# Value products of head pairs on alternating halves of the array, in four attentions, and a division moved behind a sum

## The chip, the core and the metric

One core of a Trainium2 chip runs one program from first load to last store. The metric is the device time of an execution in microseconds, median over runs; smaller is better. TensorE (PE in the profile) multiplies, VectorE (DVE), ScalarE (ACT) and GpSimd (POOL) work element by element, and SyncE (SP) issues most transfers. Each engine works through its own queue in a fixed order and waits on semaphores of the others.

## The reference

256 tokens of width 1024 pass through two transformer blocks. The first has a layer with a sparse attention of three branches (compressed, selected, windowed; 16 heads of 64 columns), a layer with a dilated attention, and a feed-forward part in each. The second block has a feed-forward part, a mixer (an index-selected attention of 8 heads, a memory attention of 4, and a state-space layer), and another feed-forward part. The part that the change touches is the end of every attention, the product of probabilities with values. In the dilated one, three groups of keys (dilations 1, 4 and 16) are joined by their log-sum-exp:

```python
def dilated_attention(h, w_q, k_shared, v_shared, w_out, rel_bias):
    ...
    for gi, (window, dilation) in enumerate(DILATIONS):
        o, lse = dilated_group_attention(q[:, :, gi], k_shared[:, :, gi], v_shared[:, :, gi], dilation, window, rel_bias)
        ...
    alpha = jax.nn.softmax(jnp.stack(lses, axis=-1), axis=-1)
    o = jnp.einsum('bsgrdi,bsgri->bsgrd', jnp.stack(outs, axis=-1), alpha)
    return o.reshape(B, S, D_MODEL).astype(h.dtype) @ w_out
```

Joined so, each head's output is the sum over the three groups of unnormalised weights times values, divided by one sum of all weights.

## The kernel before

Activations lie transposed: 128 channels on the partitions, 256 tokens along the row. Projections (`mm3`, L228 to L230) split each float32 operand into a high and a low part and make three matmuls of 128 x 128 by 128 x 256 for each block of 128 channels.

An attention works on pairs of heads. For each head the scores of two blocks of 128 queries come out of TensorE into a PSUM bank of the pool "sc" (two banks; L635 in the first attention, L766 in the dilated one). VectorE adds the position bias, keeps the row minimum and writes the result to a buffer `z` of 128 x 384 (L644, L769; one operation for 128 keys, one for 256). ScalarE makes the exponential in place and sums it (L647, L775). `pv_transposed` (L451 to L453) turns z into three blocks in a bank of the pool "tr" (two banks), and ScalarE, once in four calls of the first attention VectorE, copies them to `pt` (L458 or L456). `pv_mm` then multiplies: V is the stationary operand, 64 columns wide, so that head i of a pair fills partitions 64 i to 64 i + 63 of the output bank; two matmuls, one with 256 moving columns (L465) and one with 128 (L466). Each is in float32 and takes two passes, which are two records in the trace. Before the transposition VectorE multiplies z by the reciprocal of the sum (in the dilated attention two operations for each z, L786 and L787; z has nine buffers). At the end `split_act` splits the sum of a pair into high and low parts (L263 on ScalarE, L264 on VectorE) for the output projection.

In the first attention (`nsa`) a pair's products stand in the order head 0 branch 0, head 0 branch 1, head 1 branch 0, head 1 branch 1, and a full-width product of the compressed branch closes the bank (L694). In the dilated attention `values(h)` does one head, so three products of head 0 (one for each dilation) come before three of head 1. The index attention in `mixer` has one product for each head, and the memory attention two of 256 columns (L1196).

The program's text doesn't fix the order of the queues. A scheduler that knows dependencies and buffers moves instructions; so projections of later heads and, towards the end of an attention, the output projection stand between the attention's steps in TensorE's queue. The compression's hidden layer (`hidden`, L580) is the one place where the kernel before writes products for both halves in alternation.

Of the kernel before, what the change touches and what calls it, by code (L numbers as in the profile page):

```python
# [11 lines left out]
F32 = mybir.dt.float32  # L12
F32R = mybir.dt.float32r
AF = mybir.ActivationFunctionType
ALU = mybir.AluOpType
# [106 lines left out]
class Builder:  # L122
# [344 lines left out]

    def evac_k(self, dst, ps, R):
        self.nc.vector.tensor_tensor(dst, ps, R, ALU.mult)
# [30 lines left out]
    def nsa(self, xs, first):  # L500
# [6 lines left out]
        with ExitStack() as es:  # L507
# [173 lines left out]
            def values(g, st, j):  # L681

                den = st["den"][:, 2 * j:2 * j + 2]
                nc.vector.reciprocal(den, den)
                nc.vector.tensor_tensor(den, den, Gv[:, :, 4 * g + 2 * j:4 * g + 2 * j + 2, 1:3].rearrange("p t h b -> p h b t"), ALU.mult)
                Op = self.bank("ov")[:, :S]
                for i in range(2):
                    for br in range(2):
                        z = st["P"][2 * j + i, br]
                        nc.vector.tensor_scalar(z[:, 0:128], z[:, 0:128], den[:, i, br, 0:1], None, ALU.mult)  # L690
                        nc.vector.tensor_scalar(z[:, 128:384], z[:, 128:384], den[:, i, br, 1:2], None, ALU.mult)
                        pt = self.pv_transposed(ap, z, br + 2 * i)
                        self.pv_mm(Op, i, [Vs[:, br, tb, 64 * g:64 * g + 64] for tb in range(2)], pt, br == 0, False)
                nc.tensor.matmul(Op, Vc[:, g, 2 * j:2 * j + 2, :].rearrange("p i d -> p (i d)"), st["pc"], start=False, stop=True, skip_group_check=True)  # L694
                O.append(self.split_act(Op, "o", 2 * g + j, flip=True))
# [36 lines left out]
    def dilated(self, xs):  # L732
        nc, tc, A = self.nc, self.tc, self.A
        (XK, XQ), R, r = self.norm_all(xs, ["kv_norm", "norm_mix1"])
        with tc.tile_pool(name="dil", bufs=1) as ap:
# [5 lines left out]
            Q, O, Z, Op = {}, [], {}, [None]  # L741
# [38 lines left out]
            def values(h):  # L780
                g, i = h // 4, h % 2
                zs, rden = Z.pop(h)
                if i == 0:
                    Op[0] = self.bank("ov")[:, :S]
                for d, z in enumerate(zs):
                    nc.vector.tensor_scalar(z[:, 0:128], z[:, 0:128], rden[:, 0:1], None, ALU.mult)  # L786
                    nc.vector.tensor_scalar(z[:, 128:384], z[:, 128:384], rden[:, 1:2], None, ALU.mult)  # L787
                    pt = self.pv_transposed(ap, z, d)
                    self.pv_mm(Op[0], i, [V[:, d, tb, 64 * g:64 * g + 64] for tb in range(2)], pt, d == 0, d == 2)
                if i:  # L790
                    O.append(self.split_act(Op[0], "o", h // 2, flip=True))
# [11 lines left out]
            for h in range(17):  # L803
                if h < 16:
                    scores(h)
                    if h % 4 < 3 and h < 12:
                        queries(h // 4 + 1, h % 4)
                if h:
                    values(h - 1)
# [275 lines left out]
    def mixer(self, xs):  # L1085
# [4 lines left out]
        with ExitStack() as es:  # L1090
# [81 lines left out]
            for p in range(2):  # L1172
# [9 lines left out]
                V.reciprocal(st[:, 1], st[:, 1])  # L1182
                for i in range(2):
# [9 lines left out]
                    o = Op[64 * i:64 * i + 64]  # L1193
                    for kb in range(2):
                        h = 2 * p + i
                        nc.tensor.matmul(o, MV[:, kb, 64 * h:64 * h + 64], pt[:, kb * S:kb * S + S], start=(kb == 0), stop=(kb == 1), skip_group_check=True)  # L1196
# [24 lines left out]
            for p in range(4):  # L1221
# [15 lines left out]
                V.reciprocal(st[:, 1, :], st[:, 1, :])  # L1237
                for i in range(2):
# [3 lines left out]
                    pt = self.pv_transposed(ap, z, i, 512)  # L1242
                    self.pv_mm(Op, i, [VA[:, tb, :] for tb in range(2)], pt, True, True)
# [163 lines left out]
```

## Time and profile before

| what | us |
|---|---|
| median of 3 runs | 1373.02 (1370.69 to 1375.62) |
| the profiled execution, its time | 1374.24 |
| its span in the trace | 1372.4 |
| PE busy, share of the span | 1349.5, 98% |
| VectorE busy | 1020.7, 74% |
| ScalarE busy | 743.8, 54% |
| GpSimd busy | 186.8, 14% |

The rows come from four views: the page (engine totals and 40 slices of the span), the busy time of each engine by stretch, groups of instructions by line and shape, and the timeline of single instructions. A start in the timeline is where the record starts; a matmul's end is modelled and overlaps its follower, so spacing is read from one start to the next. Before the change the first attention's value products lie between 76 and 147 us, the dilated one's between 424 and 548, the memory and index attentions' between 1083 and 1135.

### The profile page before, as it was taken

What the parts mean: (1) busy time and instruction counts of PE and PEld (TensorE: products, weight loads), DVE (VectorE), ACT (ScalarE), POOL (GpSimd) and SP (SyncE); (2) the same over time, 40 slices, a digit from 0 to 9 for tenths busy, and PEclk for the clock granted to TensorE, in tenths of its full rate; (3) what the DMA queues carried; (4) which work ended last, traced back from release to release, by engine and by line L of the source; (5) the groups of instructions that cost most, each with busy time, mean ns of one, the idle gap of its engine ahead of it and who ended that gap; (6) DMA issues with size and microseconds to landing.
All of it is one profiled execution on the core that took longest, in us unless ns stands there. A gap on an engine that the chain in (4) does not pass through costs nothing.

```text
span 1372.4 us, 27451 instructions
## 1 busy us (share of the span) xinstructions
PE 1349.5 (98%) x10880; PEld 1277.6 (93%) x10880; DVE 1020.7 (74%) x2207; ACT 743.8 (54%) x1406; POOL 186.8 (14%) x225
## 2 busy tenths in 40 slices
PE   8999999999999999999999999999999999999997
PEld 8887999999999887899999999999987879999997
DVE  7888677766799874999954877756598797777643
ACT  4677555545668775664544555544333665554442
POOL 4200100001210000332100310001031044000011
PEclk8999999999999999999999999999999999999998
DMA  9751355546764440456755466556744254555461
GB/s 285 250 177 35 105 195 189 188 139 196 235 214 139 139 139 2 146 192 216 237 192 189 160 209 203 188 169 186 237 131 146 78 169 155 183 188 188 151 197 47
DMA packets 227120, 232.76 MB, mean 170 GB/s; under 512 B 5944, under 2 KB 221184, under 8 KB 226992
## 3 DMA queue, kind: packets, MB, share of 16 engines
q1 hardware_dynamic: 223392, 226.14, 51.9%
q10 hardware_dynamic: 3600, 4.88, 1.0%
q8 instruction: 85, 1.39, 0.4%
q14 instruction: 43, 0.35, 0.1%
HBM read 226.69 MB, written 4.30 MB: 168 GB/s over the span
## 4 chain that ended last, share of the span: by engine, by line
PE 55%; DVE 4%; issue 1%; ACT 1%; DMA 1%; POOL 0%; POOLq 0%; DVEq 0%; ACTq 0%
PE mm L228 7%; PE mm L230 7%; PE mm L229 7%; PE tr L230 4%; PE sc L230 4%; PE sc L229 4%; PE tr L228 4%; PE sc L228 4%; PE tr L229 4%; PE ov L229 2%; PE ov L230 2%; PE ov L228 2%; PE ov L1007 1%; DVE wl L188 1%; DMA mem<-in_memT_dram 1%
## 5 line engine op out<-in xcount | busy, mean ns | idle before, releaser
L187 ACT ACTIVATE wh<-raw 128x1024 fp32r<-128x1024 f32 (+2 forms) x405 | 417.9, 1036 | 452.8 <-PE mm L229 157.1
L188 DVE TENSOR_TENSOR wl<-raw,wh 128x1024 fp32r<-128x1024 f32 (+2 forms) x405 | 489.7, 1211 | 162.6 <-ACT wh L187 157.9
L228 PE MATMUL mm<-xh,wh 128*128 128x256 f32 x952 | 271.9, 286 | 1.6 <-ACT wh L187 1.4
L230 PE MATMUL mm<-xh,wl 128*128 128x256 f32 x952 | 271.2, 285 | 1.0 <-DVE wl L188 1.0
L229 PE MATMUL mm<-xl,wh 128*128 128x256 f32 x952 | 270.1, 284 | 0.0
L228 PEld LDWEIGHTS mm<-xh,wh 128*128 128x128 f32 x952 | 182.1, 191 | 7.1 <-issue 5.0
L230 PEld LDWEIGHTS mm<-xh,wl 128*128 128x128 f32 x952 | 181.2, 190 | 4.8 <-issue 3.1
L229 PEld LDWEIGHTS mm<-xl,wh 128*128 128x128 f32 x952 | 181.6, 191 | 2.5 <-issue 2.4
L293 POOL TENSOR_TENSOR sqacc<-sqacc,sq 128x256 f32<-128x256 f32 x60 | 60.8, 1016 | 613.5 <-ACT sq L292 336.4
L228 PE MATMUL sc<-xh,wh 128*128 128x256 f32 x464 | 129.8, 280 | 1.9 <-ACT wh L187 1.9
L229 PE MATMUL sc<-xl,wh 128*128 128x256 f32 x464 | 129.6, 279 | 0.0
L230 PE MATMUL sc<-xh,wl 128*128 128x256 f32 x464 | 129.3, 279 | 0.0
L228 PE MATMUL tr<-xh,wh 128*128 128x256 f32 x440 | 123.2, 280 | 0.4 <-ACT wh L187 0.4
L230 PE MATMUL tr<-xh,wl 128*128 128x256 f32 x440 | 123.3, 280 | 0.2 <-DVE wl L188 0.2
L229 PE MATMUL tr<-xl,wh 128*128 128x256 f32 x440 | 123.1, 280 | 0.0
L228 PEld LDWEIGHTS sc<-xh,wh 128*128 128x128 f32 x464 | 87.7, 189 | 2.1 <-ACT wh L187 2.1
L229 PEld LDWEIGHTS sc<-xl,wh 128*128 128x128 f32 x464 | 87.7, 189 | 0.0
L230 PEld LDWEIGHTS sc<-xh,wl 128*128 128x128 f32 x464 | 87.2, 188 | 0.0
L228 PEld LDWEIGHTS tr<-xh,wh 128*128 128x128 f32 x440 | 83.4, 189 | 0.6 <-ACT wh L187 0.6
L229 PEld LDWEIGHTS tr<-xl,wh 128*128 128x128 f32 x440 | 83.5, 190 | 0.0
L230 PEld LDWEIGHTS tr<-xh,wl 128*128 128x128 f32 x440 | 83.1, 189 | 0.4 <-DVE wl L188 0.4
L228 PE MATMUL ov<-xh,wh 128*128 128x256 f32 x224 | 62.6, 280 | 0.0
(483 smaller groups left out, 3467.2 us busy)
## 6 DMA issues: line engine op xcount, KB each, us to landing
raw<-in_ffn_w_up_dram SPq DMA_DIRECT2D x44, 1024.0 KB, 5.3
raw<-in_ffn_w_in_dram SPq DMA_DIRECT2D x44, 1024.0 KB, 5.2
raw<-in_w_in_dram SPq DMA_DIRECT2D x17, 1024.0 KB, 5.4
raw<-in_ffn_w_down_dram SPq DMA_DIRECT2D x16, 1024.0 KB, 5.3
raw<-in_ffn_w_out_dram SPq DMA_DIRECT2D x16, 1024.0 KB, 5.9
raw<-in_b_w_q_dram SPq DMA_DIRECT2D x12, 1024.0 KB, 5.2
raw<-in_a_w_in_dram SPq DMA_DIRECT2D x8, 1024.0 KB, 8.6
bt<-u_scratch SPq DMA_DIRECT2D x28, 256.0 KB, 3.8
```

The costliest lines, as they stand in the source:

```text
L187: nc.scalar.activation(hv, v, AF.Copy)
L188: nc.vector.tensor_tensor(lv, v, hv.bitcast(F32), ALU.subtract)
L228: nc.tensor.matmul(ps, sh, mh, start=(i == 0), stop=False)
L229: nc.tensor.matmul(ps, sh, ml, start=False, stop=False)
L230: nc.tensor.matmul(ps, sl, mh, start=False, stop=(i == n - 1))
L293: nc.gpsimd.tensor_tensor(acc[:, 0], acc[:, 0], s, ALU.add)
L1007: nc.tensor.matmul(o, self.s5_zc[:, s, c, :], x, start=(i == 0), stop=(i == 3), tile_position=(0, 32 * b))
```

## The change

Three things are done. A new function `pv_pair` takes both heads' `pt` and issues, for each block of keys, head 0 and then head 1, that is, left half and right half of the array in turn. The first, the index and the memory attention call it (or the same order written out) once both heads' blocks are transposed. In the dilated attention `values` now handles a pair: the two heads' transpositions of the next dilation are written ahead of the products of this one, z is no longer multiplied by the reciprocal, and at the end the two reciprocals are spread over 64 partitions each by four small matmuls, copied to `Rd` by ScalarE, and multiplied into the sum by VectorE (`od`), which is then split. `Rd` and `od` come from the two "kt" buffers that the query evacuation also uses.

```diff
+    def pv_pair(self, O, V, pts, start, stop):
+
+        nc = self.nc
+        for kb, (q0, q1, c0) in enumerate(((0, 256, 0), (128, 256, 256))):
+            for i, pt in enumerate(pts):
+                nc.tensor.matmul(O[64 * i:64 * i + 64, q0:q1], V[kb], pt[:, c0:c0 + q1 - q0], start=(start and kb == 0), stop=(stop and kb == 1), skip_group_check=True)
...
-                for i in range(2):
-                    for br in range(2):
+                ptss = []
+                for br in range(2):
+                    pts = []
+                    for i in range(2):
                         z = st["P"][2 * j + i, br]
                         nc.vector.tensor_scalar(z[:, 0:128], z[:, 0:128], den[:, i, br, 0:1], None, ALU.mult)
                         nc.vector.tensor_scalar(z[:, 128:384], z[:, 128:384], den[:, i, br, 1:2], None, ALU.mult)
-                        pt = self.pv_transposed(ap, z, br + 2 * i)
-                        self.pv_mm(Op, i, [Vs[:, br, tb, 64 * g:64 * g + 64] for tb in range(2)], pt, br == 0, False)
+                        pts.append(self.pv_transposed(ap, z, br + 2 * i))
+                    ptss.append(pts)
+                for br in range(2):
+                    self.pv_pair(Op, [Vs[:, br, tb, 64 * g:64 * g + 64] for tb in range(2)], ptss[br], br == 0, False)
...
-            def values(h):
-                g, i = h // 4, h % 2
-                zs, rden = Z.pop(h)
-                if i == 0:
-                    Op[0] = self.bank("ov")[:, :S]
-                for d, z in enumerate(zs):
-                    nc.vector.tensor_scalar(z[:, 0:128], z[:, 0:128], rden[:, 0:1], None, ALU.mult)
-                    nc.vector.tensor_scalar(z[:, 128:384], z[:, 128:384], rden[:, 1:2], None, ALU.mult)
-                    pt = self.pv_transposed(ap, z, d)
-                    self.pv_mm(Op[0], i, [V[:, d, tb, 64 * g:64 * g + 64] for tb in range(2)], pt, d == 0, d == 2)
-                if i:
-                    O.append(self.split_act(Op[0], "o", h // 2, flip=True))
+            def values(p):
+
+                g = p // 2
+                (z0, r0), (z1, r1) = Z.pop(2 * p), Z.pop(2 * p + 1)
+                Op = self.bank("ov")[:, :S]
+
+                def turned(d):
+                    return [self.pv_transposed(ap, z[d], 0) for z in (z0, z1)]
+
+                pts = turned(0)
+                for d in range(3):
+                    nxt = turned(d + 1) if d < 2 else None
+                    self.pv_pair(Op, [V[:, d, tb, 64 * g:64 * g + 64] for tb in range(2)], pts, d == 0, d == 2)
+                    pts = nxt
+                ps = self.bank("tr")[:, :S]
+                for tb in range(2):
+                    for i, r in enumerate((r0, r1)):
+                        nc.tensor.matmul(ps[64 * i:64 * i + 64, tb * P:tb * P + P], r[:, tb:tb + 1].to_broadcast([P, 64]), self.ident, start=True, stop=True, skip_group_check=True)
+                Rd = ap.tile([P, S], F32, name=self.n("Rd"), tag="kt", bufs=2)
+                nc.scalar.activation(Rd, ps, AF.Copy)
+                o = ap.tile([P, S], F32, name=self.n("od"), tag="kt", bufs=2)
+                nc.vector.tensor_tensor(o, Op, Rd, ALU.mult)
+                O.append(self.split_act(o, "o", p, flip=True))
...
-            for h in range(17):
-                if h < 16:
-                    scores(h)
-                    if h % 4 < 3 and h < 12:
-                        queries(h // 4 + 1, h % 4)
-                if h:
-                    values(h - 1)
+            for h in range(16):
+                scores(h)
+                if h % 4 < 3 and h < 12:
+                    queries(h // 4 + 1, h % 4)
+                if h and h % 2 == 0:
+                    values(h // 2 - 1)
+            values(7)
```

The memory and the index attention are changed in the same manner: both heads' `pt` first, then key block by key block with the heads in turn.

What the scheduler made of it is shown by the built order of both kernels. TensorE in the first attention, the products of one head pair (`pt` are the transposed probabilities, `Vsw` the values of both branches); before:

```order
L465 MATMUL ov_1155<-pt_1162,Vsw 64x256
L466 MATMUL ov_1155<-pt_1162,Vsw 64x128
L465 MATMUL ov_1155<-pt_1172,Vsw 64x256
L466 MATMUL ov_1155<-pt_1172,Vsw 64x128
L465 MATMUL ov_1155<-pt_1182,Vsw 64x256
L466 MATMUL ov_1155<-pt_1182,Vsw 64x128
L465 MATMUL ov_1155<-pt_1192,Vsw 64x256
L466 MATMUL ov_1155<-pt_1192,Vsw 64x128
L694 MATMUL ov_1155<-pc_870,Vc 128x256
```

and after:

```order
L473 MATMUL ov_1155<-pt_1162,Vsw 64x256
L473 MATMUL ov_1155<-pt_1170,Vsw 64x256
L473 MATMUL ov_1155<-pt_1162,Vsw 64x128
L473 MATMUL ov_1155<-pt_1170,Vsw 64x128
L473 MATMUL ov_1155<-pt_1178,Vsw 64x256
L473 MATMUL ov_1155<-pt_1186,Vsw 64x256
L473 MATMUL ov_1155<-pt_1178,Vsw 64x128
L473 MATMUL ov_1155<-pt_1186,Vsw 64x128
L705 MATMUL ov_1155<-pc_870,Vc 128x256
```

Before, pt_1162 and pt_1172 are head 0 and the other two head 1; after, neighbours in the list are head 0 and head 1.

TensorE near the end of the dilated attention, one dilation of one head pair, with the output projection (`oh`, `ol`) around it. Before, one head's product and the next one's transposition:

```order
L465 MATMUL ov_6777<-pt_6855,Vd 64x256
L466 MATMUL ov_6777<-pt_6855,Vd 64x128
L451 MATMUL tr_6871<-con,z_6761 128x128
L452 MATMUL tr_6871<-con,z_6761 128x128
L453 MATMUL tr_6871<-con,z_6761 128x128
```

and after:

```order
L473 MATMUL ov_6800<-pt_6817,Vd 64x256
L230 MATMUL sc_6966<-oh_6582,wl_6963 128x256
L228 MATMUL sc_6966<-oh_6720,wh_6962 128x256
L229 MATMUL sc_6966<-ol_6721,wh_6962 128x256
L451 MATMUL tr_6835<-con,z_6743 128x128
L452 MATMUL tr_6835<-con,z_6743 128x128
L453 MATMUL tr_6835<-con,z_6743 128x128
L473 MATMUL ov_6800<-pt_6823,Vd 64x256
L473 MATMUL ov_6800<-pt_6817,Vd 64x128
L473 MATMUL ov_6800<-pt_6823,Vd 64x128
```

The pair's four products stand in two pieces: head 0 with 256 columns by itself, then, behind other work, the other three.

## Rows read from the trace of the kernel before

**Rows 1.** The page: engine totals, and the granted clock of TensorE in 40 slices.
```profile
PE 1349.5 (98%) x10880; PEld 1277.6 (93%) x10880; DVE 1020.7 (74%) x2207; ACT 743.8 (54%) x1406; POOL 186.8 (14%) x225
...
PEclk8999999999999999999999999999999999999998
```

**Rows 2.** Busy time by stretch (length, then PE, PEld, DVE, ACT, POOL, clock, DMA, GB/s).
```profile
60.00:147.00 87.00, 85.85 (x626) 70.08 (x625) 69.53 (x279) 60.55 (x181) 6.98 (x14) 1.00 0.36 115
108.00:120.00 12.00, 10.96 (x70) 7.57 (x70) 10.96 (x54) 10.07 (x40) 0.91 (x3) 1.00 0.27 88
424.00:548.00 124.00, 123.20 (x876) 101.68 (x876) 88.82 (x346) 86.46 (x266) 0.48 (x2) 1.00 0.35 101
548.00:600.00 52.00, 46.45 (x362) 44.27 (x362) 50.58 (x162) 34.56 (x61) 20.98 (x28) 0.93 0.49 157
```

**Rows 3.** Groups by shape, TensorE, whole span: dilated (Vd) and first attention (Vsw).
```profile
L465 PE MATMUL ov<-pt,Vd 128*64 128x256 f32 x96 | 30.3, 403 | 0.3 <-ACT pt L458 0.3
...
L465 PE MATMUL ov<-pt,Vsw 128*64 128x256 f32 x64 | 17.2, 397 | 0.0
```

**Rows 4.** Timeline (start, length, engine, line) of TensorE, one call, dilated attention.
```profile
430.92 0.28 PE L229 MATMUL mm<-xl,wh 128*128 128x256 f32 x1
431.04 0.28 PE L230 MATMUL mm<-xh,wl 128*128 128x256 f32 x1
431.25 0.65 PE L465 MATMUL ov<-pt,Vd 128*64 128x256 f32 x2
431.73 0.38 PE L466 MATMUL ov<-pt,Vd 128*64 128x128 f32 x2
432.04 0.33 PE L451 MATMUL tr<-con,z 128*128 128x128 f32 x1
```

**Rows 5.** Timeline of TensorE, four calls of a head pair, first attention.
```profile
96.14 0.38 PE L466 MATMUL ov<-pt,Vsw 128*64 128x128 f32 x2
96.36 0.65 PE L465 MATMUL ov<-pt,Vsw 128*64 128x256 f32 x4
96.79 0.44 PE L466 MATMUL ov<-pt,Vsw 128*64 128x128 f32 x4
97.07 0.59 PE L465 MATMUL ov<-pt,Vsw 128*64 128x256 f32 x2
97.50 0.38 PE L466 MATMUL ov<-pt,Vsw 128*64 128x128 f32 x2
```

**Rows 6.** Timeline of TensorE, two heads next to each other, index attention.
```profile
1120.44 0.66 PE L465 MATMUL ov<-pt,VA 128*64 128x256 f32 x4
1120.93 0.40 PE L466 MATMUL ov<-pt,VA 128*64 128x128 f32 x4
1121.25 0.70 PE L1232 MATMUL sc<-KA,qa 128*128 128x256 f32 x2
```

**Rows 7.** Timeline of TensorE, the hidden layer's two halves in alternation.
```profile
50.49 0.38 PE L580 MATMUL ov<-raw,blkk 128*60 128x256 f32 x1
50.50 0.38 PE L580 MATMUL ov<-raw,blkv 128*60 128x256 f32 x1
50.71 0.38 PE L580 MATMUL ov<-raw,blkk 128*60 128x256 f32 x1
```

**Rows 8.** Groups by shape, VectorE, 424 to 548 us (busy us, mean ns).
```profile
L787 DVE TENSOR_SCALAR z<-z,rden 128x256 f32<-128x256 f32 x43 | 14.9, 347 | 0.0
L769 DVE CUSTOM_DVE_ANT_0 z<-sc,bt,mst 128x256 f32<-128x256 f32 x27 | 12.9, 478 | 0.0
...
L786 DVE TENSOR_SCALAR z<-z,rden 128x128 f32<-128x128 f32 x43 | 12.1, 281 | 0.3
L769 DVE CUSTOM_DVE_ANT_0 z<-sc,bt,mst 128x128 f32<-128x128 f32 x27 | 9.4, 347 | 10.9 <-PE sc L766 10.8
...
L489 DVE TENSOR_TENSOR qt<-mm,Rn 128x256 f32<-128x256 f32 x14 | 5.9, 421 | 2.1 <-PE mm L230 2.0
```

**Rows 9.** Groups by shape, ScalarE, 424 to 548 us (busy us, mean ns).
```profile
L458 ACT ACTIVATE pt<-tr 128x384 f32<-128x384 f32 x46 | 21.8, 485 | 21.1 <-PE tr L453 21.0
```

More of the change, by code (lines that the diff above doesn't have):

```diff
@@ L740, in dilated @@
             V = ap.tile([P, 3, 2, S], F32, name="Vd")
-            Q, O, Z, Op = {}, [], {}, [None]
+            Q, O, Z = {}, [], {}
             def queries(g, d):
@@ L1182, in mixer @@
                 V.reciprocal(st[:, 1], st[:, 1])
+                pts = []
                 for i in range(2):
@@ L1192, in mixer @@
                     nc.scalar.activation(pt, ps, AF.Copy)
-                    o = Op[64 * i:64 * i + 64]
-                    for kb in range(2):
+                    pts.append(pt)
+                for kb in range(2):
+                    for i, pt in enumerate(pts):
                         h = 2 * p + i
-                        nc.tensor.matmul(o, MV[:, kb, 64 * h:64 * h + 64], pt[:, kb * S:kb * S + S], start=(kb == 0), stop=(kb == 1), skip_group_check=True)
+                        nc.tensor.matmul(Op[64 * i:64 * i + 64], MV[:, kb, 64 * h:64 * h + 64], pt[:, kb * S:kb * S + S], start=(kb == 0), stop=(kb == 1), skip_group_check=True)
                 OM.append(self.split_act(Op, "om", 4 + p))
@@ L1237, in mixer @@
                 V.reciprocal(st[:, 1, :], st[:, 1, :])
+                pts = []
                 for i in range(2):
@@ L1241, in mixer @@
                     V.tensor_scalar(z[:, 128:384], z[:, 128:384], st[:, 1, 2 * i + 1:2 * i + 2], None, ALU.mult)
-                    pt = self.pv_transposed(ap, z, i, 512)
-                    self.pv_mm(Op, i, [VA[:, tb, :] for tb in range(2)], pt, True, True)
+                    pts.append(self.pv_transposed(ap, z, i, 512))
+                self.pv_pair(Op, [VA[:, tb, :] for tb in range(2)], pts, True, True)
                 OA.append(self.split_act(Op, "oa", p, flip=True))
```

## The prediction

> **What bounds the kernel now.** I began with the page's engine table and the clock row [rows 1]: TensorE is marked busy for 98% of 1372.4 us, at full clock in nearly every slice. That share alone doesn't prove a bound, since the end of a matmul is modelled. So I read the stretches that the change touches [rows 2]: the first attention's value products fall in 60 to 147 us (PE busy 85.85 of 87.00), the dilated one's in 424 to 548 (123.20 of 124.00). Whatever else is slow there, TensorE's queue nearly always has something to run, because projections are slotted between the attention steps. In the dilated stretch VectorE is busy 88.82 and ScalarE 86.46 us of 124: full but not the limit. Inside the first attention VectorE is close to a limit: 10.96 of 12.00 us from 108 to 120. So a microsecond taken from TensorE is a microsecond of the kernel, as long as the two evacuating engines follow.
>
> The third view is the timeline of single matmuls. One value product call in the dilated attention [rows 4]: the projection before it starts at 431.04, 0.12 after its forerunner; the call starts 0.21 later, not 0.12; its four records (two passes of 256 columns, two of 128) hold TensorE until the transposition starts at 432.04, so 0.79. Passes without a border around them cost less: 97.07 to 97.50 is 0.43 for two of 256, 96.14 to 96.36 is 0.22 for two of 128 [rows 5]. So a call is **0.65 us of passes and 0.14 + 0.09 = 0.23 us for entering and leaving** the 64-column form.
>
> What does a second call on the other half cost? Three places answer. In rows 5, heads of both halves meet in the middle: from 96.36 to 97.07, 0.71 us, lie four records of 256 and four of 128, two whole calls. In the index attention two heads happen to stand together [rows 6]: 1120.44 to 1121.25, 0.81 for two calls, against 0.79 for one. And the compression's hidden layer, written in alternation, starts its two halves 0.01 apart, every 0.22 us [rows 7]. The second half is nearly free, if it stands next in the queue.
>
> **The change part by part.** *TensorE, pass time.* I went through the built order of both kernels and cut it into unbroken runs of value calls; a run costs the longer of its two halves, at 0.43 for 256 columns and 0.22 for 128, plus 0.23.
>
> First attention: before, 32 calls x 0.65 = 20.8 (64 records of 256 columns are 32 calls) [rows 3], less five places where the halves already meet (5 x 0.65 = 3.25), so 17.6, in 18 runs (4.1): 21.7. After, 15 runs of 2, 3, 3, 8, 4, 4, 8, 5, 3, 8, 4, 1, 3, 5, 3 products (now one matmul each). Two alternating ones cost 0.43, three or four 0.65, eight 1.30, five 1.08, one 0.43: 12.1, plus 15 x 0.23 = 3.4: 15.5. **Saved: 6.2.**
>
> Dilated: before, 48 calls x 0.65 = 31.2 (96 records) [rows 3], no two halves ever together, 45 runs (10.4): 41.6. After, 24 pairs, but the order leaves nearly every one in two pieces: the first head's 256 columns alone, other work, then the other three products. That is 0.43 + 0.65 = 1.08 a pair and 26.0 in all, not 24 x 0.65 = 15.6. The broadcast of the reciprocals adds four matmuls of 128 columns a head pair, two on each half: 0.43 if alone, nothing where one half is idle anyway. In seven of the eight pairs they share a run with the lone product, so 0.4 in all. With 40 runs (9.2): 35.6. **Saved: 6.0.**
>
> Second block: index attention, 8 calls (four pairs of heads), two pairs already together: 3.9 to 3.5; memory attention (four heads, 0.86 each) 2.6 to 2.2; 9 runs before and after. **Saved: 0.8.** TensorE's sum: 13.0.
>
> *VectorE.* The dilated attention loses 48 scalings of 128 x 256 (347 ns) and 48 of 128 x 128 (281 ns) [rows 8]: 30.1 us; it gains eight products of 128 x 256 out of PSUM, for which the nearest row is the query evacuation, 421 ns: 3.4. That is 26.7 us off an engine that was not last: I take 0 for it. Its ends: if a PE wait hides behind VectorE there, at most the 0.8 us that PE stood idle in the stretch, and none is lost.
>
> *ScalarE.* Eight copies of 128 x 256 more; the 128 x 384 copy takes 485 ns [rows 9], so at most 3.9 us, against 37.5 us in which it stands idle. I take 0; without that cover, 3.9.
>
> *Waits that are added.* First, all four transpositions of a pair in the first attention now precede its products, and there are two PSUM banks for them. In two or three more places than before a third transposition follows two others and waits for the first one's copy, 0.49 us. With VectorE at 91% there, some of the saving turns into waiting for it. I take 2.0 lost; the ends are 0 and the whole 6.2.
>
> Second, in the dilated attention both heads of a pair and the next pair's first head hold all nine score buffers, so the odd head's scores can be written only after this pair's transpositions. The order shows 16 score evacuations on VectorE that wait for a transposition; behind them the TensorE queue reaches the next scores that need that bank. The round trip is 0.3 for the transposition's end (0.33 [rows 4]) plus the two score operations, 0.48 + 0.35 [rows 8]: 1.1. In 14 of the 16 the queue has more than that to do. In two only one set of four score products lies between (4 x 0.12), so 0.65 each; and near the end one row of three transpositions costs 0.5. I take 1.8; the ends are 0 and 16 x 0.65 = 10.4.
>
> Third, the evacuated sum and the broadcast share two buffers with the query evacuations; a query behind them waits for the split, about three operations of 0.4. It has 24 projection products (2.8 us) of cover each time: 0 taken, 1.2 at most in each of six pairs.
>
> Second block: its products wait for VectorE more often than they run; of 0.8 I count 0.2. **Net: 13.0 - 2.0 - 1.8 - 0.6 = 8.6 us.** A profile like the one shown (1374.24 us, 1.2 above the median) would come to 1365.6; from the median of 1373.02 it is **1364.4 us**.
>
> **Rivals.** (A) The forecast. (B) *Everything is kept.* The waits named above are covered, 13.0 us, and the hand-over after the dilated attention gets easier, because VectorE arrives there early: at 548 to 600 PE is busy 46.45 of 52.00 us and the granted clock is 0.93 [rows 2], some 7 us at 1.2 GHz in place of 2.4. If that is spared, 3.6 more: 1356 to 1360. For it: VectorE is freed. Against it: the order there, with last sums, then small VectorE steps, then weight splits, is the same as before.
>
> (C) *The evacuating engines take over.* In the first attention VectorE keeps its load, the score buffers bite oftener than twice, and 4 us or less are left: 1369 to 1375, no difference to be told. For it: 91% on VectorE, ScalarE at 70% with more to do.
>
> (D) *Slower, by the score buffers.* One mechanism: the round trip of 1.1 us stands uncovered behind all 16 evacuations. 10.4, with 4 for the two banks and 2.6 elsewhere, is 17.0 against 13.0: 1377 to 1380. It decides from 0.65 us lost per evacuation. Against it: 14 of the 16 have other products queued behind them.
>
> (E) *The halves don't run side by side in this order.* A product's two passes stand ahead of the other half's first pass; if TensorE kept to that, each run of four would cost 0.22 more. With all runs gone through so, pass time is 50.2 us, not 44.1, and the gain 8.6 - 6.1 = 2.5: 1370.5. Rows 6 speak against it, since all four records of 256 columns lie in 0.49 us there, as one call's two do in rows 4. The Trainium skill has this rule: "TensorE: Matmul & The Clock Gate", in Part 3, says matmuls start and end strictly in program order, with nothing overtaken. By that rule rows 6 would show nearly twice the time; they don't, and the measurement decides.
>
> **How the numbers follow.** A measurement of this kernel tells about 0.3%, 4.1 us, from no change. A 0.50, B 0.20, C 0.19, D 0.07, E 0.04. Faster by over 0.3% (below 1368.9): A and B and a little of C, 0.73. Slower (above 1377.1): D, 0.07. The rest, 0.20, is the same. The likeliest case is A, 1364.4, by itself 1361 to 1368. The range takes in most of B (its low end needs the clock back) and C's first half: 1358 to 1372, with about one in twenty below it and three in twenty above.
>
> **What would show it.** Right: in the dilated stretch the three-product runs last about 0.65 + 0.14 us and the lone ones 0.43 + 0.14; runs of eight in the first attention 1.4; the first attention's last value product about 4 us earlier, the dilated one's last about 8; VectorE's busy time some 27 us less. Wrong: TensorE idle in front of the score products with VectorE's score operations as releaser (C, D); transpositions waiting for copies; a run of four at 1.0 (E). And I am wrong if the stages behind 600 us, which the change does not touch, move by more than 2 us.

## The result and the profile after

The changed kernel takes 1362.58 us (median of 4 runs, 1361.33 to 1365.27) against 1373.89 for the kernel before beside it: a ratio of 0.9923, 95% interval 0.9904 to 0.9943, or some 11 us less. A second set of runs gave 1364.55 against 1376.39, 0.9921 (0.9897 to 0.9945). 1364.4 with a range of 1358 to 1372 was forecast, so the time was right. One execution of dil_only (1641 us) and one of z10 (3345 us) lie far outside all others and stand in no ratio below. The profiled execution took 1365.27, its span is 1363.5 us, 8.9 below the profiled one before.

The page and the busy time by stretch, as in [rows 1, 2]:

```profile
PE 1336.2 (98%) x10944; PEld 1266.6 (93%) x10944; DVE 1003.5 (74%) x2119; ACT 746.7 (55%) x1414; POOL 185.2 (14%) x225
...
108.00:120.00 12.00, 9.82 (x72) 6.64 (x69) 11.80 (x59) 10.15 (x40) 0.91 (x3) 1.00 0.27 88
424.00:548.00 124.00, 120.97 (x940) 99.03 (x938) 74.68 (x279) 90.79 (x273) 2.98 (x6) 1.00 0.35 99
548.00:600.00 52.00, 50.44 (x421) 50.04 (x422) 50.85 (x152) 34.73 (x62) 20.84 (x24) 0.97 0.55 178
```

Three things are to be seen. From 108 to 120 us PE is busy 9.82 of 12.00 (10.96 before), while VectorE has gone from 10.96 to 11.80: TensorE waits more there now. In the dilated stretch VectorE lost 14.1 us of work and PE 2.2; the stretch is no longer wholly the dilated attention, which ends 6 us earlier. In the hand-over PE is busy 50.44 (46.45 before) at a granted clock of 0.97 (0.93).

TensorE's timeline shows what the edit was made for, in single pieces of its queue (start, length, engine, line). First the piece of three and the lone product in the dilated attention, then a piece with the broadcasts (L808), then the piece of eight in the first attention; a piece's cost is read from its start to its follower's:

```profile
430.74 0.86 PE L473 MATMUL ov<-pt,Vd 128*64 128x256 f32 x6
431.54 0.39 PE L228 MATMUL mm<-xh,wh 128*128 128x256 f32 x1
...
433.21 0.65 PE L473 MATMUL ov<-pt,Vd 128*64 128x256 f32 x2
433.79 0.39 PE L777 MATMUL sc<-KH,q 128*128 128x256 f32 x1
...
436.16 0.87 PE L473 MATMUL ov<-pt,Vd 128*64 128x256 f32 x8
436.87 0.61 PE L808 MATMUL tr<-con,rden 128*64 128x128 f32 x8
437.40 0.39 PE L777 MATMUL sc<-KH,q 128*128 128x256 f32 x1
...
118.00 1.52 PE L473 MATMUL ov<-pt,Vsw 128*64 128x256 f32 x16 [0.51 <-DVE ol L264]
119.45 0.70 PE L705 MATMUL ov<-pc,Vc 128*128 128x256 f32 x2
```

The piece of three lasts 0.80 us (0.79 forecast), the lone product 0.58 (0.57), the piece of eight 1.45 (1.4). One call of one head took 0.79 before [rows 4].

For all that follows I use two stretches that every kernel has, both from TensorE's starts: **A**, the first attention, from its first score product (L635 before, L642 after) to its last product with Vc (L694, L705), and **D**, the dilated attention, from its first score product (L766, L777) to the last output projection product with `oh` and `wh` (L228) in an "mm" bank. The rows are those that list an operation's count, durations, first and last start; before, then after:

```profile
L635 PE MATMUL sc<-KH,q x32: 274/386/583, 49.2 to 127.6; 128*128 128x256 f32 x16, 128*128 128x512 f32 x16
L694 PE MATMUL ov<-pc,Vc x16: 377/379/484, 91.1 to 147.1; 128*128 128x256 f32 x16
L766 PE MATMUL sc<-KH,q x96: 274/283/390, 395.4 to 527.5; 128*128 128x256 f32 x96
L465 PE MATMUL ov<-pt,Vd x96: 379/379/431, 424.6 to 546.7; 128*64 128x256 f32 x96
L228 PE MATMUL mm<-oh,wh x32: 276/281/432, 106.3 to 563.8; 128*128 128x256 f32 x32
```

```profile
L642 PE MATMUL sc<-KH,q x32: 276/386/582, 50.2 to 128.6; 128*128 128x256 f32 x16, 128*128 128x512 f32 x16
L705 PE MATMUL ov<-pc,Vc x16: 377/379/483, 93.1 to 145.6; 128*128 128x256 f32 x16
L777 PE MATMUL sc<-KH,q x96: 274/283/390, 393.4 to 520.9; 128*128 128x256 f32 x96
L473 PE MATMUL ov<-pt,Vd x192: 272/352/431, 429.2 to 540.3; 128*64 128x256 f32 x96, 128*64 128x128 f32 x96
L228 PE MATMUL mm<-oh,wh x32: 276/276/393, 106.7 to 558.1; 128*128 128x256 f32 x32
```

A goes from 97.8 to 95.4 us, D from 168.3 to 164.8 (worked out from starts to 0.01 us). (D doesn't end with the last value product, since in the changed kernel 16 projection matmuls stand behind it that stood ahead of it before.) The rest is the span less A and D. In the table, "queue" is the sum over all pieces of 64-column value and broadcast products in the dilated attention, each counted from its forerunner's start plus that one's usual spacing to its follower's start. Each ratio is to the runs of the kernel before in the same set, whose medians lie between 1372.98 and 1376.39; it is not the quotient of two medians of the table.

| kernel | median | ratio to before (95%) | A | D | queue in D | rest |
|---|---|---|---|---|---|---|
| before | 1373.89 | | 97.8 | 168.3 | 41.8 | 1106.3 |
| after | 1362.58 | 0.9923 (0.9904 to 0.9943) | 95.4 | 164.8 | 36.9 | 1103.3 |
| after_again | 1364.55 | 0.9921 (0.9897 to 0.9945) | 95.0 | 164.8 | 36.9 | 1103.6 |
| nsa_only | 1371.60 | 0.9983 (0.9964 to 1.0002) | 95.3 | 167.7 | 41.8 | 1105.9 |
| dil_again | 1371.41 | 0.9971 (0.9958 to 0.9985) | 97.8 | 164.9 | 36.9 | 1107.3 |
| pair_scaled | 1367.94 | 0.9962 (0.9948 to 0.9976) | 94.3 | 162.9 | 34.2 | 1107.5 |
| div_only | 1375.64 | 1.0009 (0.9994 to 1.0025) | 94.0 | 173.5 | 46.3 | 1104.2 |
| z10 | 1367.00 | 0.9938 (0.9916 to 0.9959) | 95.2 | 166.0 | | 1103.8 |
| second_first | 1352.94 | 0.9836 (0.9797 to 0.9876) | 92.4 | 155.2 | 25.9 | 1102.4 |
| sf_adj | 1354.51 | 0.9847 (0.9819 to 0.9875) | 91.3 | 155.7 | | 1105.3 |
| sf_scaled | 1345.20 | 0.9788 (0.9767 to 0.9808) | 91.7 | 151.6 | 21.5 | 1099.7 |
| sf_act | 1344.43 | 0.9789 (0.9759 to 0.9819) | 89.8 | 154.8 | 25.8 | 1097.6 |
| sf_both | 1344.67 | 0.9794 (0.9774 to 0.9814) | 89.4 | 150.8 | | 1102.4 |

The rest differs by 10 us between kernels that are the same there but for the mixer's attentions (0.7 us after, 1.4 in the second_first kernels). Where most of that comes from stands in the last section. A single edit is therefore read from A, D and the queue first, and from the time second.

### The profile page after: what moved, and what is told of

It is laid out like the page before. It is cut to its first block, busy times and chain, and to the rows that moved or that the text cites. A ratio compares the mean times of both kernels' runs of the same rounds, so it can differ in the third digit from the quotient of the medians.

```text
span 1363.5 us, 27489 instructions
## 1 busy us (share of the span) xinstructions
PE 1336.2 (98%) x10944; PEld 1266.6 (93%) x10944; DVE 1003.5 (74%) x2119; ACT 746.7 (55%) x1414; POOL 185.2 (14%) x225
## 4 chain that ended last, share of the span: by engine, by line
PE 85%; DVE 8%; DMA 2%; issue 2%; ACT 1%; POOL 1%; SPq 0%; POOLq 0%; DVEq 0%; ACTq 0%
PE mm L228 10%; PE mm L230 10%; PE mm L229 10%; PE tr L230 6%; PE tr L228 6%; PE tr L229 6%; PE sc L230 6%; PE sc L228 6%; PE sc L229 5%; PE ov L473 3%; PE ov L228 3%; PE ov L230 3%; PE ov L229 3%; DVE wl L188 3%; PE sc L777 2%
## 5 line engine op out<-in xcount | busy, mean ns | idle before, releaser
L188 DVE TENSOR_TENSOR wl<-raw,wh 128x1024 fp32r<-128x1024 f32 (+2 forms) x405 | 491.9, 1217 | 167.4 <-ACT wh L187 162.9
L228 PE MATMUL mm<-xh,wh 128*128 128x256 f32 x952 | 270.9, 285 | 2.4 <-ACT wh L187 2.4
L228 PEld LDWEIGHTS mm<-xh,wh 128*128 128x128 f32 x952 | 181.2, 190 | 9.7 <-issue 5.3
L228 PE MATMUL sc<-xh,wh 128*128 128x256 f32 x464 | 129.7, 279 | 1.8 <-ACT wh L187 1.8
L228 PE MATMUL tr<-xh,wh 128*128 128x256 f32 x440 | 122.8, 279 | 0.0
L228 PEld LDWEIGHTS sc<-xh,wh 128*128 128x128 f32 x464 | 87.6, 189 | 2.0 <-ACT wh L187 2.0
L228 PEld LDWEIGHTS tr<-xh,wh 128*128 128x128 f32 x440 | 83.1, 189 | 0.0
L228 PE MATMUL ov<-xh,wh 128*128 128x256 f32 x224 | 62.7, 280 | 0.0
```

The costliest lines, as they stand in the source:

```text
L188: nc.vector.tensor_tensor(lv, v, hv.bitcast(F32), ALU.subtract)
L228: nc.tensor.matmul(ps, sh, mh, start=(i == 0), stop=False)
```

## The experiments

**The two attentions apart.** nsa_only is the kernel before with this one edit:

```diff
-                for i in range(2):
-                    for br in range(2):
...
+                for br in range(2):
+                    self.pv_pair(Op, [Vs[:, br, tb, 64 * g:64 * g + 64] for tb in range(2)], ptss[br], br == 0, False)
```

> Only the first attention's value products are paired; the other three attentions are as before. My theory (the halves run side by side, 6.2 us of TensorE's queue, less some 2.0 of new waits): 4.2 us less than before, a ratio near 0.997, and the trace has the first attention's last value product 4 us earlier, measured against its first score product. Rival (the evacuating engines take the saving there): 0 to 2 us less, ratio 0.9985 to 1.0, with more TensorE idle time behind transpositions and in front of value products than the 1.7 us of before.

dil_only is the kernel before with the new `values(p)` and its loop:

```diff
-            def values(h):
...
+            def values(p):
...
+                if h and h % 2 == 0:
+                    values(h // 2 - 1)
+            values(7)
```

> Only the dilated attention is changed (pairs and the division behind the sum). My theory: 6.0 us of passes less, 1.8 lost in score buffers, so 4.2; and the hand-over after it may give 1 to 2 more through the clock: ratio 0.9955 to 0.997. Rival (the first attention brings most of it): under 2 us, ratio above 0.9985. If the two single changes add up to the whole, the mixer's share is below 1.5 us.

It took 1371.88 us against 1375.35, 0.9984 (0.9971 to 0.9998): by the time, the theory's range is missed and the rival's just missed too. The same kernel was run again as dil_again:

> dil_only once more, for a trace that can be read. If the single changes add up, its dilated stretch (first score product to the last product of the output projection's first half) is 164.5 to 165 us as in the changed kernel, against 168.3 before, the first attention's and the mixer's are those of before, and its time is 3 to 5 us below before. Rival (the dilated attention profits from what the first one does): its dilated stretch is 166.5 or more.

Its time, 0.9971 (0.9958 to 0.9985), is at the theory's edge; the two runs of one kernel differ by nearly 2 us. In the stretches the two edits add up: nsa_only has the A of the changed kernel (95.3; 95.4 and 95.0) and nearly the D of before, dil_again the reverse (D 164.9; 164.8). So the first attention gave 2.5 us in these traces and the dilated one 3.5, and neither helps the other. The first is between theory and rival, the second near the theory. In time the two ratios multiply to 0.9954, with the mixer's 0.7 us to 0.995, where the whole change has 0.992: some 4 us are unaccounted for by this sum, whose two ratios each have an interval of 2 to 3 us to either side, and 2 to 4 us stand in the rest of the traces (1103.3 and 1103.6 against 1105.9 and 1107.3), the mixer's among them.

**Pairing without the division, and the division without pairing.** pair_scaled:

```diff
                 def turned(d):
+                    for z, r in ((z0, r0), (z1, r1)):
+                        nc.vector.tensor_scalar(z[d][:, 0:128], z[d][:, 0:128], r[:, 0:1], None, ALU.mult)
+                        nc.vector.tensor_scalar(z[d][:, 128:384], z[d][:, 128:384], r[:, 1:2], None, ALU.mult)
                     return [self.pv_transposed(ap, z[d], 0) for z in (z0, z1)]
...
-                Rd = ap.tile([P, S], F32, name=self.n("Rd"), tag="kt", bufs=2)
-                nc.scalar.activation(Rd, ps, AF.Copy)
-                o = ap.tile([P, S], F32, name=self.n("od"), tag="kt", bufs=2)
-                nc.vector.tensor_tensor(o, Op, Rd, ALU.mult)
-                O.append(self.split_act(o, "o", p, flip=True))
+                O.append(self.split_act(Op, "o", p, flip=True))
```

> The changed kernel, but the dilated attention scales z by the reciprocal before the transposition as in the kernel before, and has no broadcast, no Rd and no od: pairing without the division behind the sum. My theory (TensorE is the bound, VectorE's 30 us lay beside it): within 2 us of the changed kernel, ratio to before 0.991 to 0.994. Rival (the relief of VectorE is what made the dilated stretch faster): 4 us or more slower than the changed kernel, ratio above 0.995, and the last dilated value product back near its old place.

div_only puts the division behind the products of `pv_mm`, head by head:

```diff
+                for d, z in enumerate(zs):
+                    pt = self.pv_transposed(ap, z, d)
+                    self.pv_mm(Op[0], i, [V[:, d, tb, 64 * g:64 * g + 64] for tb in range(2)], pt, d == 0, d == 2)
```

> The changed kernel, but the dilated products head by head as before (three dilations of one head, then of the other), with the division behind the sum kept. My theory: the 6.0 us of passes come back, the broadcasts cost some 1, and the 1.8 of the score buffers goes: about 5 us slower than the changed kernel, ratio to before near 0.996. Rival (the relief of VectorE is what counts): within 1.5 us of the changed kernel, ratio 0.991 to 0.9935.

D decides this. Pairing alone is 5.4 us shorter than before and 1.9 shorter than the changed kernel; the division alone is 5.2 longer than before. The queue says why: without the broadcasts it is 2.7 us shorter than the changed kernel's, and div_only's is 4.5 longer than before. VectorE's 27 us bought nothing in D. In time pair_scaled missed its expectation: 0.9962 is on the rival's side, so by the time alone the rival would have won. Its D speaks against that, and its rest is 4.2 us longer than the changed kernel's; the last section shows of what. div_only came out worse than either theory said, since I had not priced its broadcasts as pieces of their own.

**Second head first.** In 17 of the 24 dilated pairs of the changed kernel the first head's 256 columns stand apart from the other three products, because its block is ready earlier. Turning the two heads round takes that freedom away:

```diff
-            for i, pt in enumerate(pts):
+            for i, pt in reversed(list(enumerate(pts))):
```

> The changed kernel, but in each block of keys the second head's product is written before the first head's. The second head's block comes out of the transposition last, so nothing of a pair can be issued ahead, and in the built order nearly all pairs of all attentions but the memory one stand in one piece of four. My theory (a product alone costs 0.43 plus 0.23 for entering and leaving, and nothing if it runs beside the other half): 24 x 0.66 less in the dilated attention, less 2 to 3 for broadcasts that now stand alone, 1.0 less in the first and 1.4 less in the index attention: some 12 to 14 us of TensorE's queue below the changed kernel, of which 9 or more show (1350 to 1355). Rival (other engines bound the dilated stretch by now): 0 to 4 us below the changed kernel, and TensorE idle behind ScalarE's copies or VectorE's score operations.

It came as expected: 1352.94 us, 23 below before, with 24 whole pieces in the dilated attention and the queue at 25.9 (36.9 less 11.0). D fell by 9.6 of those 11.0; up to the last value product, with the same number of matmuls in it, the dilated attention fell from 146.9 to 136.0, by 10.9. A fell by 3.0, the index attention by another 0.7. So TensorE's queue was still the bound. This version, one line away, gives twice the gain of the change.

**Is it the alternation?** sf_adj keeps the second head first, but writes its two products before the other head's two:

```diff
-        for kb, (q0, q1, c0) in enumerate(((0, 256, 0), (128, 256, 256))):
-            for i, pt in reversed(list(enumerate(pts))):
+        for i, pt in reversed(list(enumerate(pts))):
+            for kb, (q0, q1, c0) in enumerate(((0, 256, 0), (128, 256, 256))):
```

> As second_first, but not in alternation: both products of the second head, then both of the first, next to each other. My theory (what counts is that the other half's passes stand within about four passes in the queue): within 2 us of second_first, a piece of four at 0.79 to 0.9 us. Rival (only alternation lets the halves run side by side, passes go in program order): a piece of four costs 0.43 to 0.65 more, 39 pairs, 15 to 25 us slower than second_first and slower than the changed kernel.

The timeline of one piece of four and its follower, in sf_adj and in second_first:

```profile
473.87 0.88 PE L473 MATMUL ov<-pt,Vd 128*64 128x256 f32 x8
474.68 0.39 PE L230 MATMUL mm<-xh,wl 128*128 128x256 f32 x1
```

```profile
474.05 0.87 PE L473 MATMUL ov<-pt,Vd 128*64 128x256 f32 x8
474.85 0.39 PE L230 MATMUL mm<-xh,wl 128*128 128x256 f32 x1
```

0.81 and 0.80 us. Eight passes take about as long as one head's four (0.79 [rows 4]), in either order, so alternation isn't needed; standing next to each other is. In sf_adj the first pass of the second half starts 0.01 us after that of the first, though three other passes are written ahead of it.

**A buffer more.** z10 has ten score buffers:

```diff
-                    z = ap.tile([P, 384], F32, name=self.n("z"), tag="z", bufs=9)
+                    z = ap.tile([P, 384], F32, name=self.n("z"), tag="z", bufs=10)
```

> The changed kernel with ten score buffers instead of nine in the dilated attention (no more fit). My theory (two uncovered round trips of 0.65 each and some 0.5 of a transposition row): 0 to 1.8 us below the changed kernel, and VectorE's score operations wait for transpositions 8 us less (before the edit 8.3 us of its idle time there are put down to them). Rival (the score buffers cost TensorE much more): 4 us or more below.

The groups of VectorE's score operations with the idle time ahead of them, 393 to 541 us, in the changed kernel and in z10:

```profile
L780 DVE CUSTOM_DVE_ANT_0 z<-sc,bt,mst 128x128 f32<-128x128 f32 x32 | 11.1, 348 | 8.8 <-PE sc L777 5.5 <-PE tr L453 3.0
...
L780 DVE CUSTOM_DVE_ANT_0 z<-sc,bt 128x128 f32<-128x128 f32 x16 | 4.6, 288 | 10.6 <-PE tr L453 5.3 <-PE sc L777 5.1
```

```profile
L780 DVE CUSTOM_DVE_ANT_0 z<-sc,bt,mst 128x128 f32<-128x128 f32 x32 | 11.1, 348 | 15.9 <-PE sc L777 13.5 <-PE tr L453 2.2
...
L780 DVE CUSTOM_DVE_ANT_0 z<-sc,bt 128x128 f32<-128x128 f32 x16 | 4.6, 285 | 4.8 <-PE sc L777 4.7
```

VectorE's wait for transpositions fell from 8.3 us to 2.2, and became a wait for score products; D is 1.2 us longer, but behind its last value product this trace has 6.8 us at 1.2 GHz where the changed kernel's has 3.4; up to that product it takes 147.4 us against 146.9. Both the theory (0 to 1.8 us below) and the rival (4 or more below) missed in time: z10 is 1367.00, some 2 us above after_again. The score buffers cost TensorE no 4 us, and the edit itself gains nothing; that it costs something isn't shown.

**The control.** after_again is the changed kernel beside the last three:

> The changed kernel once more, beside the three that follow: 10 to 11 us below the kernel before (ratio 0.990 to 0.994) as in the first result. It gives a second trace: the first attention's stretch (first score product to last Vc product) 94 to 95.5 us against 97.8 before, the dilated one's (first score product to last value product) 146 to 148 against 151.6.

A, the time and the dilated stretch to its last value product (147.0 us) came out so.

**Two steps further.** sf_scaled is second_first with the scaling of pair_scaled:

> second_first without the division behind the sum: z is scaled by VectorE before the transposition as in the kernel before, no broadcast, no Rd, no od. My theory: 24 pieces of four at 0.90 = 21.6 us of TensorE's queue in the dilated attention against 25.9 in second_first (the broadcasts cost 0.44 inside a piece and 0.68 alone), VectorE's 27 us more lie beside it: 2 to 5 us below second_first. Rival (with the queue 11 us shorter VectorE becomes the bound and the division earns its place): 2 us or more above second_first, VectorE busy over 85% of the dilated stretch and TensorE idle behind its score operations or scalings.

Busy time in 136 us of the dilated stretch (PE, PEld, VectorE, ScalarE), second_first and then sf_scaled:

```profile
390.00:526.00 136.00, 134.47 (x1159) 120.76 (x1158) 95.59 (x327) 108.89 (x322) 0.00 (x0) 1.00 0.44 129
```

```profile
389.00:525.00 136.00, 133.92 (x1123) 120.47 (x1122) 115.64 (x425) 106.47 (x315) 1.64 (x3) 1.00 0.44 129
```

The rival's condition came about, VectorE at 85%, and not its result: D is 3.6 us shorter. PE is busy for over 98% in both. The division behind the sum costs more in D than it brings. In time sf_scaled gained more than the 2 to 5 us that were expected (0.9788 against 0.9836); 2.7 us of that is the rest, which the last section takes up.

sf_act is second_first with all of the first attention's copies on ScalarE:

```diff
-                        pts.append(self.pv_transposed(ap, z, br + 2 * i))
+                        pts.append(self.pv_transposed(ap, z, 0))
```

> second_first with all copies of transposed blocks in the first attention on ScalarE (none of its eight on VectorE: 4.4 us less there, 3.9 more on ScalarE). My theory (part of the first attention's saving waits for VectorE at 91% between 108 and 120 us): the first attention's stretch (first score product to last Vc product) 1 to 2 us shorter than in second_first, where it is 92.4. Rival (TensorE waits for the copy of a transposition's bank, whoever makes it, and ScalarE is the later one): same within 0.5, or 1 us longer.

Busy time from 108 to 120 us, second_first and then sf_act:

```profile
108.00:120.00 12.00, 10.93 (x73) 7.11 (x74) 11.88 (x61) 11.05 (x47) 0.91 (x3) 1.00 0.28 88
```

```profile
108.00:120.00 12.00, 11.66 (x88) 8.17 (x87) 11.53 (x63) 11.79 (x46) 0.91 (x2) 1.00 0.27 89
```

VectorE goes from 11.88 to 11.53, ScalarE from 11.05 to 11.79, and PE from 10.93 to 11.66 busy; A is 2.6 us shorter, more than expected. (A is 91.7 in sf_scaled, whose first attention is that of second_first, so up to 0.7 of it is scatter.) The page "TensorEngine Tiling (Array Packing)" of the Trainium skill warns in "PSUM Bottleneck" that the copies out of PSUM may be the limit once TensorE is faster (it speaks of fourfold); by this row the trace agrees for these 12 us of the first attention, and for no other stretch.

sf_both joins the two:

> second_first with both edits: scaling before the transposition in the dilated attention, and all copies of the first attention on ScalarE. If the two stages are independent (first attention 89.8 us as in sf_act, dilated 151.6 to the end of the output projection's first half as in sf_scaled), the time is 30 to 33 us below before (ratio 0.976 to 0.978, 1341 to 1344). Rival (what one saves the other loses in the hand-over after the dilated attention): no better than either of the two alone, 27 to 30 us below.

Both stretches kept their gain (89.4 and 150.8), and the time stayed at 1344.67: the rest is 2.7 and 4.8 us longer than in the two kernels it joins. That is the rival's outcome, and in the place that it named. In the hand-over, from the end of D to the second place where a norm's factor is spread over the partitions (L314), the same 295 matmuls take 37.3 us here, 34.4 in sf_act and 34.8 in sf_scaled. TensorE sits idle three times in it, 1.8 us in all (the third time 0.59, for VectorE's `wl`), where sf_act has no such wait and sf_scaled one of 0.6:

```profile
564.97 0.38 PE L299 MATMUL ov<-ones,sqacc 128*128 128x1 f32 x2 [0.61 <-POOL sqacc L293]
...
568.23 0.61 PE L299 MATMUL ov<-ones,sqacc 128*128 128x1 f32 x4 [0.62 <-ACT sqacc L289]
```

The feed-forward part behind it takes the same time in all three (91.9 us to its first product with `hh`, 67.4 from there to the mixer's preparation). Against sf_act another 1.6 us goes in the mixer's preparation, where this trace has 3.4 us at 1.2 GHz. All three beat the kernel before by 2.1%.

## Why the prediction was right, and where its terms were off

**The bound and the mechanism** stood. TensorE's queue sets the time in both stretches (second_first: 11.0 us of queue, 9.6 of D), the halves run side by side when they are neighbours, and a piece costs what [rows 4, 5] gave. Over all pieces of one, three and four products the costs are 0.67, 0.89 and 0.90 us, against 0.66 and 0.88 in my sum. So about 0.24 of each is the price of a piece, whatever is in it. (One reading of the kernel before was wrong: a piece at 450.5 us has both halves together, at 0.90, where I had found none in the dilated attention.) The page "TensorEngine Tiling (Array Packing)" of the Trainium skill, "Key Properties", says that a change of the tiling mode drains TensorE. It gives no price; these rows show one for entering and leaving, whatever its cause.

**Rival E** is out. Two calls of the same half, one behind the other, take 1.53 us in the kernel before (pieces at 424.6 and 461.9 us, counted as in the table); sf_adj's two calls of both halves cost 0.90 by the same count. By program order of passes they would cost 0.43 to 0.65 more, as that rival expected. The rule in Part 3 of "TensorE: Matmul & The Clock Gate" of the Trainium skill, that matmuls start in program order, doesn't hold here for two halves of the array.

**The dilated term** was 6.0 of passes less 1.8 of waits, 4.2 net; it measured 4.9 (41.8 to 36.9) less 1.4, the difference to the 3.5 by which D fell. The passes were 1.1 too good, almost wholly through the broadcasts. I had put them at 0.4 since they would share a run with a lone product. The sharing is there, but four of them still cost up to 0.44 in a piece (1.10 with a lone product against 0.67, 1.33 against 0.90 behind four), and where they stand between a lone product and its three, that piece of four takes 1.59. Against 24 pairs in two pieces each (24 x 1.08, and 40 pieces at 0.24) they cost about 1.4; against pair_scaled, the built kernel without them, the queue is 2.7 longer. The waits are in the trace where the order showed them:

```profile
439.61 0.28 PE L777 MATMUL sc<-KL,q 128*128 128x256 f32 x1
440.25 0.36 PE L777 MATMUL sc<-KH,q 128*128 128x256 f32 x1 [0.35 <-DVE rden L787]
...
530.97 0.27 PE L453 MATMUL tr<-con,z 128*128 128x128 f32 x1
531.56 0.33 PE L451 MATMUL tr<-con,z 128*128 128x128 f32 x1 [0.31 <-ACT pt L458]
```

From start to start, less a usual spacing, that is 0.52 and 0.48, and 0.51 for a second score product at 520.6: two round trips of the score buffers and one row of three transpositions, 1.5 us for the 1.8 that I took. The releaser is `rden`, not a score operation as I had named it, but VectorE's queue stands between: `rden` is behind the score operations that waited for their buffer, that is, for a transposition:

```profile
439.45 0.29 DVE L780 CUSTOM_DVE_ANT_0 z<-sc,bt 128x128 f32<-128x128 f32 x1 [1.28 <-PE tr L453]
...
440.01 0.15 DVE L787 TENSOR_REDUCE rden<-den 128x2 f32<-128x6 f32 x1
```

That 1.4 and 1.5 agree is partly luck. The kernel before has one such wait itself (0.73 at 522.9 us), and its D holds 6.8 us at 1.2 GHz behind the last value product, the changed kernel's 3.4. Up to the last value product the stretch goes from 151.6 to 146.9 us, 1.9 of it because 16 projection matmuls have left it; so 2.8 is gained there and 2.0 lost, of which the named waits explain 0.8 (1.5 less 0.73). The rest lies in spacings that are each under 0.2 us longer, and isn't traced further. Rival D, with 16 bare round trips, was far off.

**The first attention's term** was 4.2 net. Its queue, without a wait of 0.5 ahead of one piece, fell by 6.5 (22.3 to 15.7), as forecast (6.2), but A only by 2.5 to 3.8 over the six traces with this first attention (94.0 to 95.4): 2.7 to 4 us were lost, not 2.0. About 1.2 of it in this profile is a TensorE wait that ends at 64.7 us, ahead of all value products, which pair_scaled and div_only don't have. The others lie between 109 and 128 us, where TensorE's idle time rose from 1.0 us to 2.4 and VectorE's share to 11.80 of 12:

```profile
109.61 0.27 PE L453 MATMUL tr<-con,z 128*128 128x128 f32 x1
110.20 0.33 PE L451 MATMUL tr<-con,z 128*128 128x128 f32 x1 [0.31 <-ACT pt L458]
...
112.99 0.36 PE L642 MATMUL sc<-KH,q 128*128 128x256 f32 x1 [0.33 <-DVE mst L651]
113.19 0.27 PE L642 MATMUL sc<-KL,q 128*128 128x256 f32 x1
114.15 0.70 PE L705 MATMUL ov<-pc,Vc 128*128 128x256 f32 x2 [0.69 <-DVE pc L685]
```

A transposition waits for a copy, as forecast, but the waits for VectorE are the larger part: 0.7 us in this stretch before, 1.5 after, by score products, this Vc product and the piece at 118.00. That is rival C, in one of the two stretches. sf_act, which gave back some 2 us by taking eight copies off VectorE, supports it.

**VectorE's relief** was taken at nothing, and pair_scaled shows less than nothing: the scaling kept, D is 1.9 shorter. VectorE's instructions did shrink as forecast (30.1 us of scalings gone, 3.3 of `od` added); the page's busy time fell only 17.2, as records of neighbouring operations overlap and a microsecond counts once.

**The mixer** gave 0.7 us (0.2 forecast) between the memory attention's first score product and the output projection, most of the 0.9 that its queue gave up. **The hand-over** was taken at 0. From the end of D to the first product of L314 it takes 13.0 us before, and 11.9 in after, in after_again and in nsa_only alike, whose dilated attention is that of before; and the 3.4 us at 1.2 GHz, in place of 6.8, are in nsa_only too, while second_first, with VectorE as free as in the changed kernel, has 6.8. So rival B's mechanism is not what gave this. My test that stages behind 600 us don't move by over 2 holds in this profile: from 763 us to the end the lead grows from 7.6 to 8.9, the mixer's 0.7 in it. In after_again, the same program, it doesn't: from 600 to 763 us 2.5 us of the lead are lost, mostly to the spacing that the last section shows, and 4.0 are won back behind it, 0.7 of them the mixer's. Too small a loss in the first attention, too large a gain in the dilated one, and a kinder rest than assumed nearly cancelled: the three attentions gave 6.7 us of the 8.6 forecast, and the other 2 to 4 came from a rest that I had put at nothing. So the sum was closer than its terms, by luck.

## What to carry to other kernels

Price a change of array form as a price per unbroken piece of the queue plus its longer half, and read the pieces from the built order: who stands next to whom matters, not the order inside. If a scheduler issues what is ready first, write the operand that is ready last first, so that a pair can't be torn; that line was worth as much as the whole change. A relief of an engine that isn't waited for was worth nothing here even at 27 us, and if it puts four small products on the one that is, it costs.

## What the runs showed of the hardware that was not expected

The spacing of the same 128 x 256 projection matmul has two levels at full granted clock. In the feed-forward part behind the dilated attention, the changed kernel's two executions differ (busy by stretch, after and then after_again, matmuls in the bracket behind PE):

```profile
620.00:640.00 20.00, 20.00 (x179) 20.00 (x178) 16.29 (x50) 9.25 (x14) 3.74 (x9) 1.00 0.67 216
```

```profile
620.00:640.00 20.00, 20.00 (x172) 20.00 (x171) 16.17 (x52) 9.89 (x14) 4.33 (x9) 1.00 0.72 229
```

From start to start it is 0.113 us in one and 0.118 in the other, in one kernel, with PE busy and the clock at 1.00 in both; the level changes at a border between two projections and then stays for tens of us. From the norm behind the dilated attention to the mixer's preparation it makes 3.2 us between these two. With it and two other things the stretch from the end of D to the first head-norm product of the mixer's preparation (some 790 us) ranges from 224.5 us (sf_act: 0.113 there, no stretch at 1.2 GHz, no TensorE wait) to 234.2 (pair_scaled: 0.118, 3.4 us at 1.2 GHz, 2.5 of TensorE waits). The 4.2 us by which pair_scaled's rest is longer than the changed kernel's lie in this stretch: it is 6.4 longer there, and 2.2 shorter elsewhere. The level is also in the gap between second_first and sf_adj (0.118) and the three kernels that follow them (0.113): in the profiled executions some 4 us of what sf_scaled, sf_act and sf_both have over second_first isn't their edits'. What sets the level stays open; it isn't tied to an edit, as after and after_again show.
